# One transformer block in fp32 on one core: two projection sweeps of 16 steps rewritten as one hand-ordered pipeline of 32 steps

## Chip, cores and metric

The kernel runs on 1 core of one Trainium2 chip, as one launch. The metric is device time in microseconds (us), taken as the median of several executions. Engine names are those of the profile: PE is the matrix engine (PEld its weight loads), DVE the vector engine, ACT the scalar engine, POOL the general engine, SP the engine that issues nearly all DMAs.

## The reference

One trunk layer of a diffusion backbone: 512 latent tokens of width 2048, and 256 context tokens that only give keys and values. The conditioning vector `c` gives six shift, scale and gate vectors, `mod = silu(c) @ w_ada + b_ada`. In short:

```
h = rmsnorm(x) * (1 + scale1) + shift1
q, k, v, cb, cc, ch = split(h @ w_in)
attn = softmax attention of 8 query heads over 512 latent and 256 context keys
conv = cb * conv3(cc * ch)
x = x + gate1 * concat(rmsnorm(attn), rmsnorm(conv)) @ w_o
h2 = rmsnorm(x) * (1 + scale2) + shift2
x = x + gate2 * (silu(g) * a) @ w_down      where a, g = split(conv3(h2 @ w_up))
out = rmsnorm(x)
```

Each matrix product is made of three passes over a high and a low part of both operands (high by high, low by high, high by low), so that it comes out near full fp32 precision.

## The kernel before

Everything is held transposed: 128 channels on the partitions, 512 tokens along the free axis. The width of 2048 is 16 channel tiles (`KT`). Weights come from HBM as `wr` tiles, ACT casts them to the high part `wh` (line 107), DVE or POOL subtracts to get the low part `wl` (line 108), and PE runs three passes (`mm3s`, line 142).

The stage that the change touches is the first. Seven PSUM banks collect seven output tiles at a time while the loop runs over the 16 input tiles. **Sweep 1** (from line 339) does this with `x * scale1` for the seven query tiles before the RMS factor of a token is known; the factor is multiplied in later (line 410). **Sweep 2** (from line 399) does it with the finished `h` for two key tiles and five convolution tiles. A step of a sweep needs:

- its weights, 448 KB, a `load_w`: cast and subtraction;
- one column of `scale1` (sweep 1) or `shift1` (sweep 2) for its channel tile. This is a dot product of `c` with 1 MB of `w_ada` (`w_ap`): `columns_load` fetches it, `row_sums` does 32 small matmuls on PE (line 170), ACT copies the sums out (line 173), `row_cols` turns them with two more (line 177), and DVE adds the bias (`mod_cols`, lines 321 and 324);
- in sweep 2 a DVE product `hm = x * scale1 * rstd` (line 401) and a shift with a split into high and low, one ACT and one DVE instruction (lines 241, 242).

PE's order is written out by hand: `row_sums` of the next step, seven high by high matmuls, `row_cols`, seven with the low weights, seven with the low activations. The order of DVE and ACT is a planner's, made from modelled times. SP issues in order and waits where a buffer is not yet free. `fetch_w` and `fetch` chain the DMAs behind one another while `strict` is set, and loosely after it is cleared, which happens at the first step of sweep 2.

The other 64 columns of `mod` come from rows of `w_ada` that DVE multiplies with `sil = silu(c)`, spread over all partitions: two halves of 512 KB and two dots per row (line 181). This is `ada2`, which takes the next row from `rest`. Two rows are done in sweep 1, eight in sweep 2, 28 in the projections after it, 12 in the attention and 14 in the output projection (`merge`, one row per tile while there are any). The row tiles in the sweeps share four buffers (`ar`) with `w_ap`. `sil` itself is made at the start: `c` comes as four rows of one partition (`crow`), PE multiplies each by a column of ones (line 335), and ACT takes the SiLU (line 336).

Between the sweeps the seven banks are copied out by ACT (line 394), and the RMS factor `rx` is spread over the partitions by a PE product with `ones` (line 228).

Of the kernel before, what the change touches and what calls it, by code (L numbers as in the profile page):

```python
# [10 lines left out]
F32 = mybir.dt.float32  # L11
# [5 lines left out]
P = 128  # L17
# [33 lines left out]
def tile_hybrid_block(ctx: ExitStack, tc: tile.TileContext, a: dict, out: bass.AP):  # L51
# [251 lines left out]
    with tc.tile_pool(name="xpl", bufs=16) as xpl:  # L303
        def row(ap):
            return ap.rearrange("(o k) -> o k", o=1)

# [10 lines left out]
        def mod_cols(j, rows):  # L317
            o = gb[:, 2 * P:2 * P + 2]
            row_cols(o, rows)
            if j < 16:  # L320
                dve.tensor_scalar(out=mod2[:, j, :], in0=o, scalar1=col("b_ada", j), scalar2=None,
                                  op0=ADD)
            else:
                dve.tensor_scalar(out=mod2[:, j, :], in0=o, scalar1=b1[:, j - 16:j - 15],
                                  scalar2=col("norm1_w", j - 16), op0=ADD, op1=MUL)
# [11 lines left out]
        xt = []  # L337
        acc, rx = kraw[1], rstd_c

        def load_x(k):  # L340
            if k < KT:
                x = xpl.tile([P, T], F32, tag="x", name="x")
                fetch(x, a["x"][:, k])
                xt.append(x)

        def start_cols():
            sp.dma_start(out=cols, in_=a["cols"])
            o = COFF["b_ada"] + 16
            dve.tensor_scalar(out=b1, in0=cols[:, o:o + KT], scalar1=1.0, scalar2=None, op0=ADD)

        g0 = [psum(f"g0_{i}") for i in range(NQ)]
        gb = psum("gb")
        late.append(start_cols)
        sq = 0

        XK, SK = ({11: 3, 9: 3, 8: 3, 1: 2, 0: 2, 2: 2}, 10)
        for k in range(KT):
            if not k:
                ws = load_w(a["w_g0"][0], NQ * P)
                row_ = mod_load(16)  # L360
                load_x(0)
                sp.dma_start(out=ident, in_=a["ident"])
                mod_cols(16, row_sums(gb, row_, s32))
            sc = scale_col(k)
            x = xt[k]
            act.activation(r(hh[k]), x, AF.Identity, scale=sc)
# [12 lines left out]

            rows = row_sums(gb, row_, s32) if k + 1 < KT else None  # L380

            def between(k=k, rows=rows):
                if rows is not None:
                    mod_cols(17 + k, rows)
                else:
                    rstd_spread(q, NT, gb, rx)
            mm3s([(g0[i], k == 0, k == KT - 1, wh[:, i * P:(i + 1) * P],
                   wl[:, i * P:(i + 1) * P], hh[k], hl[k]) for i in range(NQ)], False, between)
            if k == SK:
                q = rstd_sums(acc, NT, D, gb[:, 3 * P:3 * P + 8])  # L390
        row_ = mod_load(0)
        for i in range(NQ):
            qraw[i] = big(f"q{i}")
            act.copy(qraw[i], g0[i])

        g0 = [psum(f"g1_{i}") for i in range(7)]
        gb = psum("gb")
        mod_cols(0, row_sums(gb, row_, s32))
        for k in range(KT):
            t = tmp("hm")  # L400
            dve.scalar_tensor_tensor(out=t, in0=xt[k], scalar=scale_col(k), in1=rx,
                                     op0=MUL, op1=MUL)
            shift_split(t, mod2[:, k, 0:1], hh[k], hl[k])
            wh, wl = load_w(a["w_g1"][k], 7 * P)
            if k + 1 < KT:
                row_ = mod_load(k + 1)
            if k % 2 == 1:
                ada2(1, ar4_tile)
# [920 lines left out]
```

## Time and profile before

| | |
|---|---|
| median of 3 executions | 2314.49 us (2313.19 to 2315.17) |
| the profiled execution | 2319.26 us, span of its trace 2317.5 us |
| PE busy | 2249.9 us, 97% of the span |
| DVE, ACT, POOL busy | 1219.3, 750.2, 381.3 us |
| mean granted PE clock | 0.985 of full speed |
| sweep 1 and sweep 2, first matmul of the first step to the next stage | 17.1 to 118.3 us, 127.8 to 249.9 us |

The profile is one execution as the hardware recorded it. The views used below are: busy time of each engine in chosen stretches (with the granted clock, as a part of 1, and what the DMAs moved), the instructions in order of time, who waited for whom, and groups of instructions with count and mean duration. A merged line of the timeline such as "x7" is several instructions in a row; matmuls overlap in the pipe, so the distance from start to start tells their cost, not the duration of one.

### The profile page before, as it was taken

The page shows a single profiled execution, that of the slowest core. Times are in us where ns is not written, and L with a number is a line of the kernel's source. Part 1 is how long each engine was busy: PE and PEld are TensorE (multiplying, and loading weights), DVE is VectorE, ACT ScalarE, POOL GpSimd, SP SyncE. Part 2 cuts the span into 40 slices and gives each one's busy share as a digit, 9 for nine tenths or more (in the row PEclk, how much of TensorE's full clock was granted, in tenths as well). Part 3 has the DMA queues.
Part 4 walks back from the last instruction along what each step waited for, and adds up shares of the span by engine and source line. Part 5 has one row for each costly group of instructions (what it writes and reads, how often), then busy time and mean ns, then how long its engine had stood idle before and what let it go on. Part 6 is the DMA issues. An engine that isn't in the chain of part 4 may idle for free. (4 is left out here: it accounts for less than half of the span.)

```text
span 2317.5 us, 28700 instructions
## 1 busy us (share of the span) xinstructions
PE 2249.9 (97%) x11446; PEld 1853.2 (80%) x11446; DVE 1219.3 (53%) x1683; ACT 750.2 (32%) x1028; POOL 381.3 (16%) x236
## 2 busy tenths in 40 slices
PE   9988999999999989999999999999999999999997
PEld 6766887777888767888888888888888888888887
DVE  3454557876888778643443434343443434343346
ACT  4322433334553333522323232322322232322324
POOL 0000000003444563210101010110101011110105
PEclk9989999999999999999999999999999999999999
DMA  9677778973554755433333333333233333333334
GB/s 360 242 239 256 240 227 284 304 236 116 166 178 159 270 177 172 128 96 100 92 99 100 92 99 98 94 99 100 91 100 99 92 100 95 97 100 96 96 100 155
DMA packets 110814, 350.33 MB, mean 151 GB/s; under 512 B 12756, under 2 KB 17108, under 8 KB 110680
## 3 DMA queue, kind: packets, MB, share of 16 engines
q1 hardware_dynamic: 108760, 345.88, 46.2%
q10 hardware_dynamic: 1920, 2.62, 0.4%
q8 instruction: 89, 1.46, 0.3%
q14 instruction: 45, 0.37, 0.0%
HBM read 335.60 MB, written 10.22 MB: 149 GB/s over the span
## 5 line engine op out<-in xcount | busy, mean ns | idle before, releaser
L108 DVE TENSOR_TENSOR wl<-wr,wh 128x1024 fp32r<-128x1024 f32 (+1 forms) x344 | 417.9, 1215 | 614.0 <-PE up L142 444.3
L107 ACT CAST wh<-wr 128x1024 fp32r<-128x1024 f32 (+2 forms) x392 | 405.3, 1034 | 991.4 <-PE up L142 474.6
L142 PE MATMUL up<-hh,wl 128*128 128x512 f32 x1312 | 324.0, 389 | 0.0
L142 PE MATMUL up<-hh,wh 128*128 128x512 f32 x1312 | 324.0, 389 | 0.0
L142 PE MATMUL up<-hl,wh 128*128 128x512 f32 x1312 | 324.0, 389 | 0.0
L142 PEld LDWEIGHTS up<-hh,wh 128*128 128x128 f32 x1312 | 246.3, 188 | 51.1
L142 PEld LDWEIGHTS up<-hh,wl 128*128 128x128 f32 x1312 | 246.3, 188 | 51.1
L142 PEld LDWEIGHTS up<-hl,wh 128*128 128x128 f32 x1312 | 246.3, 188 | 51.1
L1190 DVE SCALAR_TENSOR_TENSOR xs<-dn,mod,xs 128x512 f32<-128x512 f32 (+1 forms) x192 | 135.3, 705 | 225.7 <-PE dn L142 225.6
L1091 POOL TENSOR_TENSOR ua<-ua,ug 128x512 f32<-128x512 f32 x44 | 58.5, 1329 | 1103.2 <-ACT ug L1090 1103.2
L142 PE MATMUL dn<-fh,wh 128*128 128x512 f32 (+1 forms) x768 | 191.9, 372 | 0.0
L142 PE MATMUL dn<-fl,wh 128*128 128x512 f32 (+1 forms) x768 | 191.6, 371 | 0.0
L142 PE MATMUL dn<-fh,wl 128*128 128x512 f32 (+1 forms) x768 | 191.6, 371 | 0.0
L142 PEld LDWEIGHTS dn<-fh,wh 128*128 128x128 f32 x768 | 137.9, 188 | 25.0
L142 PEld LDWEIGHTS dn<-fh,wl 128*128 128x128 f32 x768 | 137.8, 188 | 24.9
L142 PEld LDWEIGHTS dn<-fl,wh 128*128 128x128 f32 x768 | 137.8, 188 | 24.9
L108 POOL TENSOR_TENSOR wl<-wr,wh 128x1024 fp32r<-128x1024 f32 (+1 forms) x48 | 116.8, 2436 | 165.8 <-ACT wh L107 113.0
L1098 POOL TENSOR_TENSOR fl<-ua,fh 128x512 fp32r<-128x512 f32 x44 | 97.6, 2218 | 38.5 <-ACT fh L1097 38.5
L217 POOL TENSOR_TENSOR rq<-rv,half 128x4 f32<-128x4 f32 (+2 forms) x11 | 15.9, 1459 | 497.7 <-DVE rv L213 494.1
L181 DVE CUSTOM_DVE_ANT_0 ar<-ar,sil,cols 128x1024 f32<-128x1024 f32 x50 | 63.9, 1279 | 45.5 <-DMA ar<-in_w_ada_dram 36.4
L181 DVE CUSTOM_DVE_ANT_0 ar<-ar,sil,acc 128x1024 f32<-128x1024 f32 x50 | 67.5, 1349 | 17.3 <-DMA ar<-in_w_ada_dram 15.5
L142 PE MATMUL pj<-hh,wl 128*128 128x512 f32 x272 | 68.1, 393 | 2.5 <-DVE wl L108 2.5
(307 smaller groups left out, 2851.3 us busy)
## 6 DMA issues: line engine op xcount, KB each, us to landing
wr<-in_w_up_dram SPq DMA_DIRECT2D x164, 512.0 KB, 3.6
ar<-in_w_ada_dram SPq DMA_DIRECT2D x100, 512.0 KB, 5.2
wr<-in_w_dn_dram SPq DMA_DIRECT2D x96, 512.0 KB, 3.5
ar<-in_w_ap_dram SPq DMA_DIRECT2D x48, 512.0 KB, 6.9
wr<-in_w_in_dram SPq DMA_DIRECT2D x40, 512.0 KB, 4.9
wr<-in_w_o_dram SPq DMA_DIRECT2D x32, 512.0 KB, 4.2
wr<-in_w_g_dram SPq DMA_DIRECT2D x32, 448.0 KB, 6.4
wr<-in_w_ada_dram SPq DMA_DIRECT2D x28, 512.0 KB, 4.7
```

The lines of the kernel that those rows point to most:

```text
L107: act.copy(r(wh[:, :n]), wr[:, :n])
L108: (eng or dve).tensor_tensor(out=r(wl[:, :n]), in0=wr[:, :n], in1=wh[:, :n], op=SUB)
L142: pe.matmul(ps, r(ops[a_]), r(ops[b_]), start=start and n == 0, stop=stop and n == 2)
L181: dve.tensor_tensor_reduce(out=wr, in0=wr, in1=s[:, si], op0=MUL, op1=ADD, scale=1.0, scalar=acc[:, i - 1:i] if i else col("b_ada", j), ac ...
L217: pool.tensor_tensor(out=q[:, i:e], in0=v[:, i:e], in1=half[:, :e - i], op=POW)
L1091: pool.tensor_tensor(out=ua, in0=ua, in1=ug, op=MUL)
L1098: pool.tensor_tensor(out=r(lo), in0=ua, in1=hi, op=SUB)
L1190: dve.scalar_tensor_tensor(out=x, in0=ps, scalar=mod[:, 80 + m:81 + m], in1=x, op0=MUL, op1=ADD)
```

## The change

- The two sweeps become one loop of 32 steps `g`. PE's order within a step stays (only step 0 starts with its seven first matmuls, before the row sums of step 1).
- DVE and ACT follow the order of the program until step 31 is done; the planner no longer places their work.
- Loads are issued three steps ahead (`w_load(g + 3)`, `mod_load(g + 3)`), all in one strict order until the end of step 31.
- The activations of step g + 1 and the cast of the weights of step g + 2 are done in step g, also where sweep 1 goes over to sweep 2. The seven banks are finished and copied out one after the other in step 15.
- Six rows of `w_ada` are done in the sweeps instead of ten: two in sweep 1, four in sweep 2. The latter four use the tiles of `x` as buffers (four DMAs of 256 KB a row), as these come free. The list `rest` goes on as before, so that the planned 28 and 12 rows follow, `merge` does 16 and the gate loop of the FFN the last two.
- `sil` is loaded by one DMA that reads `c` once for each partition, issued at step 6; ACT takes the SiLU in two halves in steps 8 and 9. The four rows, the eight matmuls and the four SiLUs at the start are gone.
- The first DMA behind `c2` is the 1 MB of `w_ap` for step 0, ahead of the first weights.

The diff, cut to what is spoken of:

```diff
-        def mod_load(j):
-            if j < 16:
-                return columns_load(a["w_ap"][j], ar4_tile, 1024)
-            if j % 2:
-                return columns_load(a["w_ap"][j], ar4_tile, 1024)
-            return columns_load(a["w_ap"][j], lambda: big("aq"), 512)
-
...
+        def w_load(g):
+            if g < 2 * KT:
+                raw[g] = wr_tile()
+                src = a["w_g0"][g] if g < KT else a["w_g1"][g - KT]
+                fetch_w(raw[g][:, :NQ * P], src)
+
+        def w_hi(g):
+            if g < 2 * KT:
+                wh = wp.tile([P, 1024], F32, tag="wh", name="wh")
+                act.copy(r(wh[:, :NQ * P]), raw[g][:, :NQ * P])
+                wt[g] = wh
+
+        def w_lo(g):
+            if g < 2 * KT:
+                wl = wp.tile([P, 1024], F32, tag="wl", name="wl")
+                n, wr, wh = NQ * P, raw.pop(g), wt[g]
+                dve.tensor_tensor(out=r(wl[:, :n]), in0=wr[:, :n], in1=wh[:, :n], op=SUB)
+                wt[g] = wh, wl
+
+        def make_hm(g):
+            if KT <= g < 2 * KT:
+                hm[g] = tmp("hm")
+                dve.scalar_tensor_tensor(out=hm[g], in0=xt[g - KT], scalar=scale_col(g - KT),
+                                         in1=rx, op0=MUL, op1=MUL)
+
+        def make_h(g):
+            k = g % KT
+            if g < KT:
+                sc = scale_col(k)
+                act.activation(r(hh[k]), xt[k], AF.Identity, scale=sc)
+                w_hi(g + 1)
+                dve.scalar_tensor_tensor(out=r(hl[k]), in0=xt[k], scalar=sc, in1=hh[k],
+                                         op0=MUL, op1=SUB)
+            else:
+                b, t = mod2[:, k, 0:1], hm.pop(g)
+                act.activation(r(hh[k]), t, AF.Identity, bias=b)
+                w_hi(g + 1)
+                make_hm(g + 1)
+                dve.scalar_tensor_tensor(out=r(hl[k]), in0=t, scalar=b, in1=hh[k],
+                                         op0=ADD, op1=SUB)
+
+        def ada_load(tile_, w):
+            j = rest.pop(0)
+            fa = sm.tile([P, 4], F32, tag="acc", name="acc")
+            fn = chain_dot(mod, j, sil, fa)
+            n = D // w
+            for i in range(n):
+                wr = tile_()
+                fetch(wr, a["w_ada"][j - 32, :, w * i:w * (i + 1)])
+
+                def dot(wr=wr, i=i):
+                    fn(wr, slice(i * w, (i + 1) * w), i, i == n - 1)
+                    if i == n - 1 and 64 <= j < 80:
+                        scale1(mod[:, j:j + 1], col("norm2_w", j - 64))
+                dots.append((dot, w))
+
+        def dot(w):
+            while dots and w >= dots[0][1]:
+                w -= dots[0][1]
+                dots.pop(0)[0]()
+
...
+        sweeps = ExitStack()
+        EN = mybir.EngineType
+        sweeps.enter_context(tc.manual_schedule(engines={EN.DVE, EN.Activation}))
...
-        crow = [big("row") for _ in range(4)]
-        for j in range(4):
-            sp.dma_start(out=crow[j][0:1, :], in_=row(a["c"][j * T:(j + 1) * T]))
-        sp.dma_start(out=pick, in_=a["pick"])
-        for j in range(4):
-            ps = psum("cb")
-            pe.matmul(ps, ones[0:1, :], crow[j][0:1, :], start=True, stop=True)
-            act.activation(sil[:, j * T:(j + 1) * T], ps, AF.Silu)
+        rows_ = {0: mod_load(0)}
+        fetch(cols, a["cols"])
+        fetch(pick, a["pick"])
+        load_x(1)
+        w_load(0)
+        rows_[1] = mod_load(1)
+        w_load(1)
+        load_x(2)
+        fetch(ident, a["ident"])
+        w_load(2)
+        rows_[2] = mod_load(2)
...
-        XK, SK = ({11: 3, 9: 3, 8: 3, 1: 2, 0: 2, 2: 2}, 10)
-        for k in range(KT):
-            if not k:
-                ws = load_w(a["w_g0"][0], NQ * P)
-                row_ = mod_load(16)
-                load_x(0)
-                sp.dma_start(out=ident, in_=a["ident"])
-                mod_cols(16, row_sums(gb, row_, s32))
-            sc = scale_col(k)
-            x = xt[k]
-            act.activation(r(hh[k]), x, AF.Identity, scale=sc)
-            dve.scalar_tensor_tensor(out=r(hl[k]), in0=x, scalar=sc, in1=hh[k], op0=MUL, op1=SUB)
-            wh, wl = ws
-            if k + 1 < KT:
-                ws = load_w(a["w_g0"][k + 1], NQ * P)
-                row_ = mod_load(17 + k)
-            for _ in range(XK.get(k, 1)):
-                load_x(len(xt))
-            if k in (11, 13):
-                ada2(1, ar4_tile)
-            while sq < len(xt) - 1 or sq < KT and len(xt) == KT:
-                add_square(acc, xt[sq], sq == 0, eng=dve)
-                sq += 1
-
...
+        mod_cols(0, row_sums(gb, rows_.pop(0), s32))
+        act.activation(r(hh[0]), xt[0], AF.Identity, scale=scale_col(0))
+        w_hi(0)
+        dve.scalar_tensor_tensor(out=r(hl[0]), in0=xt[0], scalar=scale_col(0), in1=hh[0],
+                                 op0=MUL, op1=SUB)
+        w_lo(0)
+        w_hi(1)
+
+        XN = {0: 1, 1: 1, 2: 2, 3: 2, 4: 2, 5: 2, 6: 2, 7: 1}
+        SN = {2: 3, 3: 2, 4: 2, 5: 2, 6: 2, 7: 2, 8: 2, 9: 1}
+        AD = {9: (ar4_tile, 1024), 11: (ar4_tile, 1024), 19: (x_tile, 512), 22: (x_tile, 512),
+              25: (x_tile, 512), 28: (x_tile, 512)}
+        DT = (11, 13, 21, 24, 27, 30)
+        SK, last = 10, 2 * KT - 1
+        added = 0
+        for g in range(2 * KT):
+            k = g % KT
+            if g == KT:
+                banks = [psum(f"g1_{i}") for i in range(NQ)]
+            wh, wl = wt.pop(g)
+
+            def group(n, i):
+                w, h = ((wh, hh[k]), (wl, hh[k]), (wh, hl[k]))[n]
+                pe.matmul(banks[i], r(w[:, i * P:(i + 1) * P]), r(h),
+                          start=k == 0 and n == 0, stop=k == KT - 1 and n == 2)
+
+            def group7(n):
+                for i in range(NQ):
+                    group(n, i)
+
+            if g == 0:
+                group7(0)
+            if g < last:
+                rows = row_sums(gb, rows_.pop(g + 1), s32)
+            w_load(g + 3)
+            if g + 3 <= last:
+                rows_[g + 3] = mod_load(g + 3)
+            load_x(XN.get(g, 0))
+            if g in AD:
+                ada_load(*AD[g])
+            if g == 6:
+                fetch(sil, a["c"].partition_broadcast(P))
+            w_lo(g + 1)
+            added = square_add(added)
+            if g in DT:
+                dot(1024)
+            square(SN.get(g, 0))
+            if g in (8, 9):
+                c_ = sil[:, (g - 8) * 1024:(g - 7) * 1024]
+                act.activation(c_, c_, AF.Silu)
+            group7(1 if g == 0 else 0)
+            if g < last:
+                mod_cols(g + 1, rows)
+                make_h(g + 1)
+            if g in DT:
+                dot(1024)
+            if KT < g <= KT + NQ:
+                dve.tensor_tensor(out=qraw[g - KT - 1], in0=qraw[g - KT - 1], in1=rx, op=MUL)
+            if g == SK + 1:
+                q = rstd_cols(gb[:, 3 * P:3 * P + 8:2], NT, D)
+            if g == SK + 2:
+                dg = diag(q, NT)
+            if g == KT - 1:
+                for i in range(NQ):
+                    group(1, i)
+                    group(2, i)
+                    qraw[i] = big(f"q{i}")
+                    act.copy(qraw[i], banks[i])
+                continue
+            if g:
+                group7(1)
+            if g == KT - 2:
+                pe.matmul(gb, ones, dg, start=True, stop=True)
+                act.copy(rx, gb)
+                make_hm(KT)
+            group7(2)
+            if g == SK:
+                for t in range(NT):
+                    pe.matmul(gb[:, 3 * P + 2 * t:3 * P + 2 * t + 2], acc[:, t * P:(t + 1) * P],
+                              ones[:, :2], start=True, stop=True)
+        sweeps.close()
+        strict[0] = False
+        g0 = banks
     ab = ctx.enter_context(ExitStack())
     kvp = ab.enter_context(tc.tile_pool(name="kvp", bufs=1, reuse_waits="tile"))
```

## Rows read from the trace of the kernel before

**Rows 1.** The page: busy time of PE, share of the span and instructions.
```profile
PE 2249.9 (97%) x11446; PEld 1853.2 (80%) x11446; DVE 1219.3 (53%) x1683; ACT 750.2 (32%) x1028; POOL 381.3 (16%) x236
```

**Rows 2.** Busy time by stretches: stretch, its length, engines (instructions), clock, DMA share, GB/s.
```profile
24.00:118.25 94.25, 94.00 (x802) 73.96 (x801) 45.70 (x73) 35.28 (x60) 1.01 (x1) 1.00 0.81 300
...
127.79:249.92 122.13, 106.51 (x818) 81.84 (x815) 56.20 (x87) 31.51 (x50) 0.00 (x0) 0.92 0.78 259
```

**Rows 3.** PE in order of time: start, duration, instruction, count, idle before and its releaser.
```profile
23.96 1.08 PE L170 MATMUL gb<-aq,s 128*32 128x128 f32 x32
...
30.21 1.08 PE L170 MATMUL gb<-ar,s 128*32 128x128 f32 x32
...
118.25 1.08 PE L170 MATMUL gb<-ar,s 128*32 128x128 f32 x32
...
127.79 2.82 PE L142 MATMUL g<-hh,wh 128*128 128x512 f32 x7
...
193.21 1.08 PE L170 MATMUL gb<-ar,s 128*32 128x128 f32 x16 [6.40 <-DMA ar<-in_w_ap_dram]
...
245.03 1.89 PE L142 MATMUL g<-hh,wh 128*128 128x512 f32 x7
...
249.92 1.98 PE L142 MATMUL pj<-hh,wh 128*128 128x512 f32 x8
```

**Rows 4.** Waits of PE from 0 to 250 us: total us, times, longest.
```profile
PE gb L170 <- DMA ar<-in_w_ap_dram: 16.3, 6, 6.4
PE gb L170 <- DVE mod L321: 4.4, 2, 4.0
```

**Rows 5.** DVE and ACT in order of time, between the sweeps.
```profile
117.00 3.52 ACT L394 COPY q<-g 128x512 f32<-128x512 f32 x7 [1.24 <-PE g L142]
...
120.44 4.30 DVE L410 TENSOR_TENSOR q<-q,rstd_c 128x512 f32<-128x512 f32 x7
...
125.66 0.21 DVE L321 TENSOR_SCALAR mod<-gb,cols 128x2 f32<-128x2 f32 x1
```

**Rows 6.** Waits of SP's queue, 118 to 250 us.
```profile
SPq L126 <- DVE acc L181: 32.8, 8, 5.3
```

**Rows 7.** SP and PE in order of time, start of the kernel.
```profile
2.70 7.16 PE L335 MATMUL cb<-row,ones 1*128 1x512 f32 x8 [2.70 <-DMA row<-in_c_dram]
...
3.31 0.43 SPq L126 DMA_DIRECT2D aq<-in_w_ap_dram  x1
...
9.79 2.40 PE L170 MATMUL gb<-aq,s 128*32 128x128 f32 x32
...
17.09 3.36 PE L142 MATMUL g<-hh,wh 128*128 128x512 f32 x7
```

**Rows 8.** Busy time by stretches at the start, columns as in rows 2.
```profile
4.00:10.00 6.00, 6.00 (x11) 1.86 (x14) 1.18 (x2) 2.72 (x5) 0.00 (x0) 1.00 0.87 295
...
10.00:24.00 14.00, 11.75 (x93) 7.75 (x87) 5.54 (x8) 5.82 (x10) 0.00 (x0) 1.00 1.04 400
```

**Rows 9.** DVE's groups from 0 to 420 us: count, busy us, mean ns, idle before.
```profile
L108 DVE TENSOR_TENSOR wl<-wr,wh 128x896 fp32r<-128x896 f32 x32 | 34.8, 1089 | 30.8 <-ACT wh L107 30.7
L181 DVE CUSTOM_DVE_ANT_0 ar<-ar,sil,cols 128x1024 f32<-128x1024 f32 x25 | 32.0, 1281 | 39.7 <-DMA ar<-in_w_ada_dram 30.5 <-DMA r<-kraw 9.2
...
L401 DVE SCALAR_TENSOR_TENSOR hm<-x,mod,rstd_c 128x512 f32<-128x512 f32 x16 | 11.5, 748 | 1.2 <-ACT rstd_c L238 1.0
```

**Rows 10.** DMA issues: KB each, median us from issue to landing.
```profile
ar<-in_w_ap_dram SPq DMA_DIRECT2D x48, 512.0 KB, 6.9
```

**Rows 11.** DVE's groups from 765 to 890 us, in the output projection.
```profile
L181 DVE CUSTOM_DVE_ANT_0 wr<-wr,sil,cols 128x1024 f32<-128x1024 f32 x10 | 22.7, 2273 | 6.2 <-DMA wr<-in_w_ada_dram 6.2
...
L181 DVE CUSTOM_DVE_ANT_0 wr<-wr,sil,acc 128x1024 f32<-128x1024 f32 x10 | 16.4, 1643 | 0.1
```

**Rows 12.** DVE's busy time, last row of the output projection to the row sums behind it.
```profile
840.15:858.43 18.28, 14.75 (x27) 0.92 0.40 124
```

**Rows 13.** PE in order of time, the row sums behind the output projection.
```profile
858.57 1.05 PE L232 MATMUL st<-ones,junk 128*128 128x2 f32 x8 [1.83 <-DVE junk L258]
```

More of the change, by code (lines that the diff above doesn't have):

```diff
@@ L303, in tile_hybrid_block, with mod_load @@
     with tc.tile_pool(name="xpl", bufs=16) as xpl:
-        def row(ap):
-            return ap.rearrange("(o k) -> o k", o=1)
         def scale_col(k):
             return mod2[:, 16 + k, 0:1]
-        def mod_load(j):
-            if j < 16:
-                return columns_load(a["w_ap"][j], ar4_tile, 1024)
-            if j % 2:
-                return columns_load(a["w_ap"][j], ar4_tile, 1024)
-            return columns_load(a["w_ap"][j], lambda: big("aq"), 512)
-        def mod_cols(j, rows):
+        def mod_load(g):
+            src = a["w_ap"][(16 + g) % 32]
+            if g < KT and g % 2 == 0:
+                return columns_load(src, lambda: big("aq"), 512)
+            return columns_load(src, ar4_tile, 1024)
@@ new lines, in tile_hybrid_block, with x_tile, load_x @@
+        xt, hm, wt, raw, hold, sq = [], {}, {}, {}, {}, []
+        acc, rx = kraw[1], rstd_c
+        def x_tile():
+            return xpl.tile([P, T], F32, tag="x", name="x")
+        def load_x(n):
+            for _ in range(n):
+                x = x_tile()
+                fetch(x, a["x"][:, len(xt)])
+                xt.append(x)
+        def w_load(g):
[3 more added lines that the diff above has]
+                fetch_w(raw[g][:, :NQ * P], src)
@@ new lines, in tile_hybrid_block @@
+        dots = []
+        def ada_load(tile_, w):
[11 more added lines that the diff above has]
+                dots.append((dot, w))
@@ new lines, in dot, with square @@
+        def dot(w):
+            while dots and w >= dots[0][1]:
+                w -= dots[0][1]
+                dots.pop(0)[0]()
+        def square(n):
+            for _ in range(n):
+                if len(sq) < KT:
+                    if not sq:
+                        act.activation(acc, xt[0], AF.Square)
+                        sq.append(None)
+                        continue
+                    s = tmp("sq")
+                    act.activation(s, xt[len(sq)], AF.Square)
+                    sq.append(s)
@@ L327, in tile_hybrid_block, with square_add @@
+        def square_add(n):
+            for s in sq[n:]:
+                if s is not None:
+                    dve.tensor_tensor(out=acc, in0=acc, in1=s, op=ADD)
+            return len(sq)
+        sweeps = ExitStack()
+        EN = mybir.EngineType
+        sweeps.enter_context(tc.manual_schedule(engines={EN.DVE, EN.Activation}))
         sp.dma_start(out=s2, in_=a["c2"])
-        crow = [big("row") for _ in range(4)]
-        for j in range(4):
-            sp.dma_start(out=crow[j][0:1, :], in_=row(a["c"][j * T:(j + 1) * T]))
+        rows_ = {0: mod_load(0)}
@@ L391, in tile_hybrid_block @@
[L391 to L408, printed above, removed]
-            if 1 <= k <= NQ:
-                dve.tensor_tensor(out=qraw[k - 1], in0=qraw[k - 1], in1=rx, op=MUL)
-            if k == 0:
-                strict[0] = False
-            rows = row_sums(gb, row_, s32) if k + 1 < KT else None
-            def between(k=k, rows=rows):
-                if rows is not None:
-                    mod_cols(k + 1, rows)
-            mm3s([(g0[i], k == 0, k == KT - 1, wh[:, i * P:(i + 1) * P],
-                   wl[:, i * P:(i + 1) * P], hh[k], hl[k]) for i in range(7)], False, between)
@@ new lines, in tile_hybrid_block @@
+        fetch(cols, a["cols"])
[8 more added lines that the diff above has]
+        rows_[2] = mod_load(2)
+        o = COFF["b_ada"] + 16
+        dve.tensor_scalar(out=b1, in0=cols[:, o:o + KT], scalar1=1.0, scalar2=None, op0=ADD)
+        banks = [psum(f"g0_{i}") for i in range(NQ)]
+        gb = psum("gb")
+        mod_cols(0, row_sums(gb, rows_.pop(0), s32))
```

36 lines of the change are left out of this document (7 added, 29 removed).

## The prediction

> **What bounds it now.** I began with the page: PE is busy 97% of the span [rows 1], so only time that PE stands still or runs slowly can be won. The stretches say where that lies [rows 2]. In sweep 1 PE is busy 94.00 of 94.25 us at full clock; sweep 2, with the same count of matmuls, takes 122.13 us, is busy 106.51 and has a granted clock of 0.92. PE in order of time gives the measure: a step of sweep 1 takes 30.21 - 23.96 = 6.25 us from row sums to row sums, and a last step, which has none behind it, 249.92 - 245.03 = 4.89 us [rows 3]. Row sums alone take 1.08 us. Were sweep 2 to follow at once with that period, it would end at 118.25 + 1.08 + 15 x 6.25 + 4.89 = 217.97 us; it ends at 249.92. So **32.0 us** are lost, 8.5 between the sweeps (127.79 - 118.25 - 1.08) and 23.5 in sweep 2.
>
> The waits say by whom [rows 4]. Six times PE waits for a `w_ap` load, 16.3 us in all, up to 6.40 us at 193.21 us [rows 3]; the rest of the 23.5 is the half clock behind such a stall and short waits. These loads are late because SP, in order, stands in front of a buffer that a dot of `ada2` has not yet read: 32.8 us in eight waits [rows 6], one for each of the eight rows in sweep 2. Between the sweeps DVE is the cause: it runs seven `q` scalings in a row, 4.30 us from 120.44 us, before the bias at 125.66 us for which PE waits [rows 5].
>
> The 23.5 us come from starts of matmuls, not from PE's idle time, which is 122.13 - 106.51 = 15.6 us [rows 2]; the difference is slow clock that counts as busy. (The Trainium skill, "Perfetto Trace Analysis", "Identifying the Most-Contended Engine", says that matmul busy share is no good measure of the distance to the roofline, because matmuls are pipelined. Taken by busy share, sweep 2 would give 7.9 us less and the time would be 2291.9 us; the clock of 0.92 bears the rule out here.)
>
> **The change, part by part.**
>
> *Between the sweeps.* Step 16's activations are made in step 15 and the scalings are spread one to a step, so the 8.5 us go. What is late next are ACT's seven copies, 3.52 us [rows 5], now each behind its bank's last matmuls in step 15. The copy of step 17's row sums stands behind the seventh, and the last bank is needed about when it comes free. I charge 1 us; bounds 0 and 4, the latter what one stall cost before (below).
>
> *Sweep 2.* Per step SP issues the weights and two halves of `w_ap`, three steps ahead. Four `ar` buffers hold two steps, so a pair is issued when the row sums of step g + 1 are over, 1.1 us into step g, and is needed at the start of step g + 2: 2 x 6.25 - 1.1 = 11.4 us against 6.9 us from issue to landing [rows 10]. No dot shares these buffers in sweep 2 any more. Bytes: 1.51 MB a step and 1.05 MB for a row of `w_ada` every third, 1.86 MB in 6.25 us, 297 GB/s, where the stream has reached 400 [rows 8]. The four rows wait in SP for tiles of `x`, at steps 25 and 28 until the middle of the step or of the next; behind that wait stand only loads for two steps later, at 28 those of the next stage. DVE in the fullest step (21): subtraction 1.09, two dots 2.56, bias 0.21, `hm` and the low part 0.75 each, a scaling 0.61, together 5.97 of 6.25 us [rows 5, 9]; other dot steps lack the scaling. A waiting DVE or ACT instruction now holds back all behind it on its engine, but the activations are due 3 us before PE wants them and the low parts 5. So all 23.5 us go.
>
> *Sweep 1.* It had nothing to win; its two rows still share `ar`, where SP's wait ends within the step. The SiLUs in steps 8 and 9 (no row for this shape; about two casts of half the width, 1 us each) fit beside ACT's four other instructions.
>
> *The broadcast of `c`.* No row shows such a DMA. From below 1.05 MB at 400 GB/s, 2.6 us [rows 8]; from above two loads of half the size one after the other, 2 x 6.9 = 13.8 us [rows 10]. It is issued in step 6 behind step 9's loads and needed in the middle of step 8, over 12.5 us later. I take the first, as it is 128 runs of 8 KB, hidden; at the other end it costs 1 us.
>
> *Start.* Before, PE's eight products for `sil` (7.16 us from 2.70) and SP's small loads came first, and the first `w_ap` load was issued at 3.31 us, the row sums began at 9.79 and the first step at 17.09 [rows 7], step 1 at 23.96 [rows 3]. Now `w_ap` is issued 2 us earlier, and the first matmuls don't wait for the second column. The stream ran at 295 GB/s from 4.0 us, about 1 us behind the first large issue [rows 8]; from 2.2 us it brings the 2.03 MB of column, bias, first `x` and weights by 9.1. With the activation and the cast, some 2 us, the first step starts at 11.1. Its 21 matmuls took 6.87 us with the cold clock (17.09 to 23.96), the row sums of step 1 come between them at the cold 2.40 [rows 7]: step 1 at 20.4, **3.5 us** earlier. Bounds 1 and 6 (a stream a fifth slower; warm row sums and a faster chain).
>
> *Four rows of `w_ada` put off.* The projections and the attention do as many rows as before. `merge` does 16, two more, at its end. Such a row costs DVE 2.27 + 1.64 = 3.92 us there, 7.8 for both [rows 11], and from the last dot to the row sums DVE is busy 14.75 of 18.28 us [rows 12]: 3.5 free, and PE waits 1.83 us for DVE at that point already [rows 13]. I charge **4 us**; bounds 0 (the dots slip behind the sums) and 8 (all of it). Their four loads also stand in the `wr` buffers ahead of the next weights, which is part of the upper bound. The two rows in the gate loop I cost at nothing: DVE is idle 47% of the span [rows 1]; without that cover they are 4 x 1.28 = 5.1 us [rows 9].
>
> *Sum:* 32.0 + 3.5 - 1 - 4 = **30.5 us**. The profiled execution took 2319.26 us (span 2317.5), 4.8 above the median; it would take 2288.8, the median 2314.49 - 30.5 = **2284.0**. With the bounds: 32 + 6 = 38 gives 2276.5, 32 + 1 - 4 - 8 = 21 gives 2293.5. The planner also lays the later stages anew; what that does no row tells, and I let the range carry a few us for it.
>
> **Rivals.**
>
> *Stalls at the rows (2293 to 2306).* The four rows of sweep 2 are in the strict order, 1.05 MB each, and behind them everything waits. Before, six stalls cost 16.3 us idle [rows 4] and 7.9 of slow clock, 4.0 each; four would give back 16: 2300. For it: SP's waits for dots were the cause before, and SP now waits for `hm` at steps 25 and 28. Against: the 11.4 us of lead and 297 of 400 GB/s.
>
> *Late in every step (slower).* The lead of two steps is too short: with four buffers the period is half of landing time plus 1.1 us. From a landing of 11.4 us on this costs, and from 14.9 us on (a period of 8.0, 16 x 1.8 = 28 us and the slow clock behind each stall) it eats the gain. At 17 us the period is 9.05 and the loss 45 us: 2284 + 45 = 2329. For it: DVE and ACT can no longer be moved around a late load. Against: 6.9 us [rows 10].
>
> *The order was not the cause (no change).* If loads come late for a reason in the memory, 23.5 us stay, half of the hand-over too, and the rows in `merge` eat the start: 2311. Against: sweep 1, with more bytes a second (300 against 259 GB/s [rows 2]), has no stall.
>
> **How the numbers follow.** Forecast 0.78, stalls at the rows 0.15, no change 0.03, slower 0.04. A measurement of this kernel tells 0.2% (4.6 us) from no change. Faster: 0.78 + 0.15 = 0.93; same 0.03; slower 0.04. The range takes the forecast's bounds, 3 us below for the later stages, and most of the stalls: 2273 to 2302.
>
> **What would show it.** Right: in the changed trace the row sums follow each other by 6.25 us through all 32 steps, the first at about 20 us, the projection's first matmul at about 215 us, no PE wait for `w_ap`, clock 1.00 from 24 us on, and a PE wait before the row sums behind the output projection of some 6 us instead of 1.83. Wrong: PE waits for `w_ap` at steps 21 to 31 (stalls), a period over 7 us in sweep 2 (late in every step), or a projection that starts at 215 us and a time over 2300, when later stages gave the gain back.

## The result, and the profile after

The changed kernel takes 2287.22 us (median of 4 runs, 2283.14 to 2292.19), the kernel before 2313.84 on the same chip: a ratio of 0.9885 (95% interval 0.986 to 0.9911), 1.15% faster. The forecast was 2284.0, in a range of 2273 to 2302. The profiled execution took 2292.19 us, 27.1 less than that of before (2319.26); the traces are compared against this difference.

The page, PE's line [rows 1]:
```profile
PE 2233.5 (98%) x11438; PEld 1842.9 (80%) x11438; DVE 1222.7 (53%) x1699; ACT 747.9 (33%) x1026; POOL 383.6 (17%) x236
```
Busy time by stretches, columns as in [rows 2]: step 1 to step 15, from there to the projections, then output projection, first products with `w_u`, gate loop.
```profile
18.76:108.45 89.69, 89.45 (x781) 69.93 (x780) 45.86 (x73) 36.59 (x62) 1.79 (x1) 1.00 0.88 324
108.45:213.17 104.72, 104.72 (x902) 82.57 (x902) 60.20 (x105) 35.43 (x59) 0.00 (x0) 1.00 0.85 291
706.20:814.80 108.60, 95.02 (x388) 75.65 (x386) 88.46 (x98) 29.90 (x41) 58.13 (x26) 0.93 0.70 239
814.80:894.60 79.80, 73.47 (x306) 57.59 (x306) 60.19 (x112) 29.72 (x43) 36.14 (x18) 0.98 0.51 159
894.60:987.10 92.50, 89.05 (x384) 73.25 (x385) 55.15 (x64) 40.65 (x52) 21.00 (x12) 0.98 0.44 138
```
The second line is the change's success: from step 15 on PE is busy in 104.72 of 104.72 us at full clock, where sweep 2 of before stood still and ran slowly [rows 2]. The last line is the opposite. The same stage of the kernel before, in the same view:
```profile
926.90:1014.00 87.10, 87.10 (x386) 72.14 (x385) 48.23 (x53) 40.16 (x52) 19.31 (x12) 1.00 0.38 119
```
It had no idle time there; it has 3.45 us now, and is 5.4 us longer.

PE in order of time, columns as in [rows 3]:
```profile
10.84 3.32 PE L459 MATMUL g<-hh,wh 128*128 128x512 f32 x7 [1.96 <-ACT wh L344]
14.09 1.08 PE L170 MATMUL gb<-ar,s 128*32 128x128 f32 x32
...
18.76 0.93 PE L170 MATMUL gb<-aq,s 128*32 128x128 f32 x24
...
108.45 1.08 PE L170 MATMUL gb<-ar,s 128*32 128x128 f32 x32
...
114.71 1.08 PE L170 MATMUL gb<-ar,s 128*32 128x128 f32 x32
...
202.25 1.08 PE L170 MATMUL gb<-ar,s 128*32 128x128 f32 x32
...
213.17 1.98 PE L142 MATMUL pj<-hh,wh 128*128 128x512 f32 x8
```
Step 0 begins at 10.84 us, step 1 at 18.76 and step 16 at 114.71, one period of 6.25 after step 15: no hand-over is left, and 202.25 - 114.71 is fourteen periods of 6.25. (Only step 1 and the two steps with extra products, 10 and 14, are longer: 6.74, 7.04 and 7.13 us.) The projections begin at 213.17 instead of 249.92. PE's waits from 0 to 230 us, as in [rows 4]. Of the 16.3 us for `w_ap` there 1.3 lie in step 0, at 14.89 us; the other 15.0, five waits in sweep 2, are gone (of the 5.5 here 4.21 lie ahead of the very first matmul, the rest at 5.89 and 19.92 us):
```profile
PE gb L170 <- DMA aq<-in_w_ap_dram: 5.5, 3, 4.2
PE g L459 <- ACT wh L344: 2.0, 1, 2.0
...
```

How far a profiled execution is ahead of that of before, at the start of each stage, in us:

| kernel | projections | output projection | `w_u` | `up` (gate loop) | `dn` | whole time |
|---|---|---|---|---|---|---|
| changed | 36.7 | 38.5 | 33.6 | 32.3 | 26.9 | 27.1 |
| after_again | 35.5 | 39.1 | 35.2 | 35.9 | 30.8 | 31.0 |
| gate_rows_later | 36.2 | 41.1 | 35.5 | 34.2 | 34.2 | 33.6 |
| four_rows_in_gate | 36.0 | 40.5 | 39.5 | 41.3 | 41.3 | 41.5 |
| half_merge_rows | 36.3 | 43.3 | 47.7 | 51.4 | 41.4 | 40.5 |
| rows_spread | 36.7 | 42.1 | 57.9 | 62.4 | 62.2 | 50.9 |
| rows_spread_8 | 36.9 | 38.8 | 54.0 | 57.6 | 57.7 | 46.3 |

The changed kernel wins 36.7 us in the sweeps, 1.8 more up to the output projection, and gives back 6.2 from there to the gate loop and 5.4 in it. Two profiles of this one kernel (the first two lines) differ by up to 3.9 us at a mark, and the first six lines, whose programs are the same up to the output projection, by 4.8 us there; smaller differences between two lines say nothing.

Where it gives back is seen in order of time. In the gate loop, DVE, SP and PE:
```profile
896.75 1.81 SPq L126 DMA_DIRECT2D wr<-in_w_ada_dram  x2
...
902.46 1.28 DVE L181 CUSTOM_DVE_ANT_0 wr<-wr,sil,cols 128x1024 f32<-128x1024 f32 x1 [2.99 <-DMA wr<-in_w_ada_dram]
...
906.60 0.75 DVE L242 SCALAR_TENSOR_TENSOR hl<-hm,mod,hh 128x512 fp32r<-128x512 f32 x1
907.41 0.50 PE L142 MATMUL up<-hl,wh 128*128 128x512 f32 x1 [3.43 <-DVE hl L242]
907.74 3.15 PE L142 MATMUL up<-hh,wl 128*128 128x512 f32 x8
```
A dot of `ada2` stands in DVE's order ahead of the last low part `hl`, and its load is not there yet. DVE waits 2.99 us for the row, works off its dots, then makes `hl`, for which PE has waited 3.43 us; the clock falls behind that gap (0.98 over the stage), which makes up the rest of the 5.4. This is no accident of one profile: six profiled kernels do the two rows in these passes (changed, after_again and four of the experiments below), and in each PE waits for `hl`, 2.3 to 3.6 us, and the gate loop gives back 4.3 to 6.5.

PE's waits in the three stages, 690 to 1000 us (`oa` is the output projection, `u` the products with `w_u`, `st` the row sums behind it), and ACT at the end of the output projection:
```profile
PE oa L142 <- ACT wh L107: 7.5, 3, 4.5
PE oa L142 <- POOL wl L108: 4.4, 2, 2.9
PE u L142 <- ACT wh L107: 3.9, 2, 2.2
PE up L142 <- DVE hl L242: 3.4, 1, 3.4
PE st L232 <- DVE junk L258: 2.4, 1, 2.4
```
```profile
813.91 0.83 ACT L107 CAST wh<-wr 128x768 fp32r<-128x768 f32 x1 [8.29 <-DMA wr<-in_w_u_dram]
```
In the same three stages of before these waits were:
```profile
PE oa L142 <- ACT wh L107: 6.8, 4, 2.5
PE oa L142 <- POOL wl L108: 2.5, 1, 2.5
PE u L142 <- ACT wh L107: 2.2, 1, 2.2
PE st L232 <- DVE junk L258: 1.8, 1, 1.8
```
They are each somewhat longer now, 4.9 us together, though waits of this size also differ between kernels with the same `merge` (the first is 9.6 us in before_no_rows). Most are for weights, not for the row sums: the four loads of the two further rows take turns with the weights in the `wr` buffers, and a cast for `w_u` waits 8.29 us for its load. What holds the weights up is seen in SP's queue, from 706 to 815 us:
```profile
SPq L120 <- DVE mod L181: 21.2, 10, 5.0
SPq L120 <- DVE acc L181: 16.6, 3, 8.0
```
SP waits with loads of weights (line 120) for buffers that a dot (line 181) has not read yet; before, from 745 to 848 us, these were 17.6 and 16.0 us. It is the kind of wait that the prediction saw in sweep 2.

### The profile page after: what moved, and what is told of

Same layout as the page of the kernel before. It is cut to its first block, busy times and chain, and to the rows that moved or that the text cites. A ratio compares the mean times of both kernels' runs of the same rounds, so it can differ in the third digit from the quotient of the medians.

```text
span 2290.4 us, 28675 instructions
## 1 busy us (share of the span) xinstructions
PE 2233.5 (98%) x11438; PEld 1842.9 (80%) x11438; DVE 1222.7 (53%) x1699; ACT 747.9 (33%) x1026; POOL 383.6 (17%) x236
## 5 line engine op out<-in xcount | busy, mean ns | idle before, releaser
L107 ACT CAST wh<-wr 128x1024 fp32r<-128x1024 f32 (+1 forms) x360 | 375.3, 1043 | 966.7 <-PE up L142 473.1
L108 DVE TENSOR_TENSOR wl<-wr,wh 128x1024 fp32r<-128x1024 f32 x312 | 383.8, 1230 | 575.0 <-PE up L142 436.7
L181 DVE CUSTOM_DVE_ANT_0 ar<-ar,sil,cols 128x1024 f32<-128x1024 f32 x42 | 53.8, 1281 | 33.3 <-DMA ar<-in_w_ada_dram 20.8
L142 PE MATMUL pj<-hh,wh 128*128 128x512 f32 x272 | 69.5, 397 | 0.0
```

What stands on the lines that cost most here:

```text
L107: act.copy(r(wh[:, :n]), wr[:, :n])
L108: (eng or dve).tensor_tensor(out=r(wl[:, :n]), in0=wr[:, :n], in1=wh[:, :n], op=SUB)
L142: pe.matmul(ps, r(ops[a_]), r(ops[b_]), start=start and n == 0, stop=stop and n == 2)
L181: dve.tensor_tensor_reduce(out=wr, in0=wr, in1=s[:, si], op0=MUL, op1=ADD, scale=1.0, scalar=acc[:, i - 1:i] if i else col("b_ada", j), ac ...
```

## The experiments

Theory: (1) in the kernel before, the eight rows of sweep 2, with their dots and loads in loose order, cost its 23.5 us; (2) in the changed kernel the gate loop's loss is the dot that waits for its load, not DVE's time; (3) in the output projection every row costs PE time by its loads. There are twelve runs in three groups; each ratio is to the kernel before, timed again with its group (2316.79, 2315.99 and 2316.87 us).

**after_again**: the changed kernel once more, for a second profile.

> The changed kernel once more, as the measure for the next three, which differ from it only behind the attention. Both theories: 2283 to 2292 us, median near 2287; the sweeps end near 213 us; PE waits some 3.4 us for a low part (hl) at the start of the up projections in at least some executions. Theory A: the give-back of some 10 us behind the sweeps comes from the four rows of w_ada that were put off (two in the gate loop, two in merge). Theory B: it is the scatter of those stages, whose order the planner lays anew, and the rows cost nothing by themselves.

Measured: 2287.64 us (2282.15 to 2288.26), ratio 0.9869 (0.9856 to 0.9882). The wait for `hl` is there again, 3.1 us, and the gate loop gives back 5.1. The two stages ahead of it give back 3.2 instead of 6.2.

**gate_rows_later**: the two rows of the gate loop go from its first two passes (counted 3 and 4 in the program) to passes 4 and 5.
```diff
-        ada2(-(-len(rest) // (6 - i)) if i < 6 else len(rest), wr_tile)
+        ada2(0 if i < 4 else -(-len(rest) // (6 - i)) if i < 6 else len(rest), wr_tile)
```


> The last two rows are done at i = 4 and 5 of the gate loop instead of 3 and 4, so that no dot stands in DVE's queue ahead of the last low part of h. Theory A: the PE wait of 3.4 us for hl and the slow clock behind it go, some 5 us less than the changed kernel, median near 2282. Theory B: within 2 us of the changed kernel.

Measured: 2285.78 us (2281.89 to 2287.02), ratio 0.9863 (0.985 to 0.9877). In the profile the wait for `hl` is gone and the gate loop gives back nothing (34.2 at both ends). The median is 1.9 us under after_again, with intervals that overlap: the mechanism is shown by the profile, its worth of 5 us is not shown by the times. (This profile lost 6.9 us ahead of the gate loop, more than the other two.)

**four_rows_in_gate**: as that, and the last two rows of `merge` are left to the gate loop as well.
```diff
-        ada2(1, wr_tile)
+        ada2(int(m < 14), wr_tile)
```


> As gate_rows_later, and merge does 14 rows as before the change; all four rows put off are done at i = 4 and 5 of the gate loop. Theory A: the lead over the kernel before stays 38 to 40 us from the attention to the end, another 4 to 7 us less, median near 2276. Theory B: within 2 us of the changed kernel, or the gate loop takes as much longer.

Measured: 2279.44 us (2277.38 to 2286.31), ratio 0.9844 (0.9828 to 0.986). Output projection and gate loop, columns as in [rows 2]:
```profile
704.20:808.90 104.70, 94.01 (x387) 75.68 (x386) 85.25 (x94) 30.99 (x43) 60.35 (x28) 0.94 0.69 234
...
885.60:972.70 87.10, 87.10 (x386) 72.10 (x385) 57.72 (x69) 39.05 (x52) 18.38 (x12) 1.00 0.51 164
```
The gate loop now has four rows instead of two and takes 87.10 us as before the change, without idle time, though DVE is busier (57.72 against 55.15 us). So its loss was one of order, not of DVE's time. The stages ahead of it gain 0.8 instead of losing 6.2 or 3.2.

**half_merge_rows**: `merge` does a row in every second call only; the gate loop does ten.
```diff
-        ada2(1, wr_tile)
+        ada2(m % 2, wr_tile)
...
-        ada2(-(-len(rest) // (6 - i)) if i < 6 else len(rest), wr_tile)
+        ada2({3: 0, 4: 3, 5: 3}.get(i, 4), wr_tile)
```


> merge does a row on every second tile (8 instead of 16), the other ten are done in the gate loop, three at i = 4, three at i = 5, four at i = 6. Theory A, a row in merge costs PE time because DVE is nearly full there: 8 rows less give back more than the two of four_rows_in_gate, 2264 to 2272. Rival to that: the gate loop has 8 dots per 22 us beside its own work and PE waits there instead, 2276 to 2290. Theory B: within 2 us of the changed kernel.

Measured: 2281.82 us (2277.06 to 2282.19), ratio 0.9845 (0.9831 to 0.9858), no better. From the output projection to the gate loop the lead grows by 8.1 us (43.3 to 51.4) where four_rows_in_gate had 0.8: 7.3 for six rows fewer in `merge`, 1.2 each. The gate loop then loses 10.0. Gate loop, and PE's longest waits in and behind it:
```profile
875.50:972.60 97.10, 89.53 (x384) 72.99 (x384) 73.89 (x92) 37.24 (x50) 18.07 (x12) 0.98 0.61 197
```
```profile
PE up L142 <- DVE wl L108: 5.4, 2, 3.6
...
PE dn L142 <- ACT wh L107: 2.2, 1, 2.2
```
Three and four rows a pass are too many: PE waits for the low part of a weight that DVE makes behind the dots.

**before_no_rows**: in the kernel before, sweep 2 does no row; the eight columns of `mod` are filled with ones.
```diff
-                ada2(1, ar4_tile)
+                j = rest.pop(0)
+                dve.memset(mod[:, j:j + 1], 1.0)
```


> The kernel before, without the eight rows of w_ada in sweep 2 (left out of the computation, a constant stands in their columns of mod). Theory C: SP's waits for these dots made the w_ap loads late, so PE's six waits of 16.3 us go and sweep 2 takes 99 to 103 us instead of 122; the hand-over of 9.5 us stays, and the projections start near 227 to 231 us instead of 250. Theory D: the planner's order of DVE and ACT is the cause, rows or not; sweep 2 stays above 112 us and the projections start above 238 us.

Measured: 2296.73 us (2293.47 to 2301.97), ratio 0.992 (0.9898 to 0.9942). Between the sweeps and sweep 2, columns as in [rows 2], then PE's waits, 0 to 250 us:
```profile
118.25:127.80 9.55, 3.35 (x68) 2.49 (x66) 8.72 (x15) 4.25 (x9) 0.00 (x0) 0.78 0.43 139
127.80:226.60 98.80, 98.80 (x822) 77.72 (x815) 38.09 (x55) 31.65 (x50) 0.00 (x0) 0.99 0.70 235
```
```profile
PE gb L170 <- DVE mod L321: 4.0, 1, 4.0
...
PE gb L170 <- DMA ar<-in_w_ap_dram: 1.3, 1, 1.3
```
Sweep 2 takes 98.80 us instead of 122.13: 23.3 of the 23.5 us are the rows'. The one wait for `w_ap` lies in step 0; sweep 2 has none. The hand-over stays, as nothing there was touched.

**before_strict**: in the kernel before, the fetches keep their strict order to the end of sweep 2.
```diff
-            if k == 0:
+            if k == KT - 1:
                 strict[0] = False
```


> The kernel before with the strict order of loads kept to the last step of sweep 2, all eight rows in it. If the buffers shared with dots are the cause of the stalls, they stay: sweep 2 over 112 us, projections from 240 to 252 us. Rival: the loose order let loads of later stages and of rows go ahead of w_ap; strict alone brings sweep 2 to 99 to 105 us and the start to 227 to 233 us.

Measured: 2305.45 us (2301.97 to 2310.1), ratio 0.9948 (0.9931 to 0.9964). Sweep 2, then PE's waits, 0 to 250 us, then SP's, 118 to 240:
```profile
127.80:238.30 110.50, 103.41 (x819) 79.02 (x816) 56.82 (x88) 31.12 (x51) 0.00 (x0) 0.96 0.86 306
```
```profile
PE gb L170 <- DVE mod L321: 6.8, 2, 4.8
PE gb L177 <- ACT rs L173: 3.6, 4, 1.4
PE gb L170 <- DMA ar<-in_w_ap_dram: 3.1, 4, 1.3
...
```
```profile
SPq L126 <- DVE acc L181: 34.9, 8, 6.1
```
SP waits for the dots as long as before (34.9 against 32.8 us [rows 6]), yet PE's waits for `w_ap` fall from 16.3 to 3.1 us (in sweep 2 alone from 15.0 to 1.8). The strict order alone brings the projections 11.6 us forward, half of what the rows cost. In the half that is left PE waits mostly for DVE and ACT; why these are late was not tested. Neither theory's number came out.

**rows_in_wap_buffers**: in the changed kernel the four rows share the `w_ap` buffers again.
```diff
-        AD = {9: (ar4_tile, 1024), 11: (ar4_tile, 1024), 19: (x_tile, 512), 22: (x_tile, 512),
-              25: (x_tile, 512), 28: (x_tile, 512)}
+        AD = {9: (ar4_tile, 1024), 11: (ar4_tile, 1024), 19: (ar4_tile, 1024), 22: (ar4_tile, 1024),
+              25: (ar4_tile, 1024), 28: (ar4_tile, 1024)}
```


> The changed kernel, but the four rows of sweep 2 are loaded into the four ar buffers that w_ap uses (two DMAs of 512 KB) instead of the tiles of x. Theory C: SP again waits for dots in front of w_ap loads; PE waits for w_ap some 2 to 5 us at each of the four rows, the projections start at 218 to 233 us. Rival: the strict order three steps ahead absorbs it, start at 213 to 215 us.

Measured: 2290.8 us (2289.81 to 2293.78), ratio 0.9891 (0.9871 to 0.991). PE has one wait for `w_ap` in this sweep, and the projections begin at 214.7 us. That wait, and SP's waits for the rows:
```profile
PE gb L170 <- DMA ar<-in_w_ap_dram: 1.1, 1, 1.1
```
```profile
SPq L126 <- DVE mod L181: 9.4, 3, 3.6
```
SP does stand in front of the dots' buffers again, for 9.4 us, but PE hardly feels it; whether the lead of three steps, the strict order or the smaller number of rows takes it up, this run does not tell. One step takes 7.58 us instead of 6.25: the buffers in `x` are worth 1.3 us here, not the whole gain.

**after_planner_order**: the changed kernel with DVE and ACT placed by the planner again.
```diff
-        sweeps.enter_context(tc.manual_schedule(engines={EN.DVE, EN.Activation}))
```


> The changed kernel with DVE and ACT left to the planner in the sweeps; loads, buffers and the order of the program as in the change. Theory C: loads and buffers were the cause of the stalls in sweep 2; the projections start at 213 to 221 us, at most the hand-over (some 5 us) comes back. Theory D: the fixed order is what removed them; stalls return, start at 230 us or later.

Measured: 2291.0 us (2285.1 to 2291.23), ratio 0.9887 (0.9867 to 0.9907). The period in sweep 2 stays within 0.02 us of 6.25 but for one step of 6.37, and the projections begin at 214.1 us, inside the 213.2 to 214.5 of the table's first six lines. In the sweeps the fixed order as such is worth no more than 0.1 us.

**lead_two**: loads two steps ahead instead of three.
```diff
-        w_load(2)
-        rows_[2] = mod_load(2)
...
-            w_load(g + 3)
-            if g + 3 <= last:
-                rows_[g + 3] = mod_load(g + 3)
+            w_load(g + 2)
+            if g + 2 <= last:
+                rows_[g + 2] = mod_load(g + 2)
```


> The changed kernel with loads issued two steps ahead instead of three. If the lead is what keeps PE from waiting: a w_ap load is then issued some 1 us into step g and needed at the start of step g + 1, 5.2 us against 5.4 us from issue to landing, so PE waits 0.5 to 2 us in most steps and the projections start at 220 to 250 us. Rival: the loads land in time because nothing else stands in the queue; start at 212 to 216 us.

Measured: 2290.77 us (2285.63 to 2293.12), ratio 0.988 (0.9865 to 0.9895). One place is late, 96.5 to 98.4 us, with 1.4 us in three waits; two steps are longer by 0.9 and 1.3 us, 2.2 together, and the projections begin at 215.8, 2.7 us later.

**after_old_start**: the changed kernel with the old way to `sil`.
```diff
+        crow = [big("row") for _ in range(4)]
+        for j in range(4):
+            sp.dma_start(out=crow[j][0:1, :],
+                         in_=a["c"][j * T:(j + 1) * T].rearrange("(o k) -> o k", o=1))
...
+        for j in range(4):
+            ps = psum("cb")
+            pe.matmul(ps, ones[0:1, :], crow[j][0:1, :], start=True, stop=True)
+            act.activation(sil[:, j * T:(j + 1) * T], ps, AF.Silu)
...
-            if g == 6:
-                fetch(sil, a["c"].partition_broadcast(P))
...
-            if g in (8, 9):
-                c_ = sil[:, (g - 8) * 1024:(g - 7) * 1024]
-                act.activation(c_, c_, AF.Silu)
```


> The changed kernel with sil made at the start as before (four rows of c, eight matmuls, four SiLUs), without the broadcast DMA. If the start was worth the 5.2 us that the trace shows (step 1 at 18.8 instead of 24.0 us), the first step's matmuls start at 13 to 15 us and the projections at 216 to 219 us. Rival: the small loads and products hide beside the 1 MB load that comes anyway, start within 1 us of 213 us.

Measured: 2287.74 us (2285.44 to 2289.71), ratio 0.9879 (0.9861 to 0.9896). The first matmul of step 0 comes at 14.56 us instead of 10.84, step 1 at 22.42 instead of 18.76, the projections at 216.3, 3.1 later. In after_again these are 11.37, 20.52 and 214.5, so the price lies between 1.9 and 3.7 us. In the whole time it can't be told from the changed kernel.

**rows_spread**: the rows are spread further: `merge` does six, passes 4 to 6 of the gate loop two each, the first down projection one at each of its first six steps.
```diff
-        ada2(1, wr_tile)
+        ada2(int(m in (0, 1, 4, 7, 10, 13)), wr_tile)
...
-        ada2(-(-len(rest) // (6 - i)) if i < 6 else len(rest), wr_tile)
+        ada2(2 if i in (4, 5, 6) else 0, wr_tile)
...
-            down((i - 2) // CH - 1)
+            down((i - 2) // CH - 1,
+                 hooks={m2: [lambda: ada2(1, wr_tile)] for m2 in range(6)} if i == 6 else {})
```


> The changed kernel with the 18 rows behind the attention spread anew: merge does 6 (tiles 0, 1, 4, 7, 10, 13), the gate loop two each at i = 4, 5, 6, and the first down projection six, one behind each of its first six pairs of tiles. Theory A with the price that half_merge_rows gave (about 1.7 us of PE time for each row in merge, none for two a pass of the gate loop): ten rows less in merge give 17 us on four or five rows at the start of the up projections, and nothing is lost behind them if DVE has room in the down projection; 2262 to 2272. Rival: DVE or the row loads hold up the down projection as they did the gate loop with three and four rows, 2275 to 2285.

Measured: **2269.69 us** (2268.36 to 2272.27), ratio 0.9793 (0.978 to 0.9807). This beats both kernels: 47.2 us less than the kernel before, timed with it. Output projection, `w_u`, gate loop and the beginning of `dn`:
```profile
702.60:790.50 87.90, 87.90 (x387) 72.47 (x386) 58.63 (x66) 32.84 (x45) 55.54 (x29) 1.00 0.59 192
790.50:864.50 74.00, 71.19 (x308) 56.53 (x307) 55.58 (x105) 26.83 (x38) 31.20 (x16) 1.00 0.51 158
864.50:951.80 87.30, 87.30 (x384) 72.08 (x385) 63.35 (x80) 38.04 (x51) 18.03 (x12) 1.00 0.57 184
951.80:1000.00 48.20, 41.47 (x165) 32.74 (x164) 34.89 (x46) 9.46 (x11) 2.78 (x2) 0.93 0.67 216
```
The output projection takes 87.90 us at full clock instead of 108.60, and the gate loop does six rows in 87.30. The first down projection is the new place of loss (62.2 us of lead at its start, 51.0 at its end). There PE waits 6.7 us in four waits, one of them here, in order of time:
```profile
954.14 1.28 DVE L181 CUSTOM_DVE_ANT_0 wr<-wr,sil,cols 128x1024 f32<-128x1024 f32 x1 [3.13 <-DMA wr<-in_w_ada_dram]
955.35 1.22 DVE L108 TENSOR_TENSOR wl<-wr,wh 128x1024 fp32r<-128x1024 f32 x1
956.63 2.08 PE L142 MATMUL dn<-fh,wl 128*128 128x512 f32 x4 [2.85 <-DVE wl L108]
```
It is the chain of the gate loop again: a dot waits for its row ahead of a low part.

**rows_spread_8**: as that, with eight rows in the sweeps (six of them in steps 19 to 29, every second) and four in `merge`.
```diff
-        AD = {9: (ar4_tile, 1024), 11: (ar4_tile, 1024), 19: (x_tile, 512), 22: (x_tile, 512),
-              25: (x_tile, 512), 28: (x_tile, 512)}
-        DT = (11, 13, 21, 24, 27, 30)
+        AD = {9: (ar4_tile, 1024), 11: (ar4_tile, 1024)}
+        AD.update({g: (x_tile, 512) for g in range(19, 30, 2)})
+        DT = (11, 13, 21, 23, 25, 27, 29, 31)
...
-        ada2(1, wr_tile)
+        ada2(int(m in (2, 5, 8, 11)), wr_tile)
```


> As rows_spread, with eight rows in the sweeps instead of six (one every second step from 19 to 29, loads into the tiles of x) and four in merge. DVE would be busy some 10 of 12.5 us in two steps of sweep 2 and the stream move 326 of 400 GB/s, so the sweeps should keep their period and the projections start at 213 to 215 us; two rows less in merge: 2 to 4 us under rows_spread. Rival: the loads come late, PE waits for w_ap in sweep 2 and the start is past 217 us.

Measured: 2273.0 us (2270.93 to 2277.61), ratio 0.9809 (0.9795 to 0.9823), no gain over rows_spread. The sweeps bear the two rows (projections at 213.0 us, every step of sweep 2 6.25 us), but the lead is 3.3 us smaller ahead of the output projection, within what two profiles of one kernel differ by.

## Why the prediction was right, point by point

The median came out 3.2 us above the forecast of 2284.0. That is closer than the terms are: against the profile three came out better than forecast, by 4.6 us together, and three worse, by 8.2. That they cancel to 3.6 is luck. The largest term, the 32.0 us of hand-over and sweep 2, was read from start to start of the row sums and needs no reason for the stalls; it held, while the reason given held in part. The terms, in us (their sum is 26.9, the last mark but one in the table):

| term | predicted | measured | how |
|---|---|---|---|
| hand-over and sweep 2 | 32.0 - 1 | 32.1 | step 16 to the projections: (249.92 - 119.33) - (213.17 - 114.71) |
| start | 3.5 | 5.2 | 23.96 - 18.76; 3.4 in the second profile |
| sweep 1 | 0 | -0.6 | step 1 to 16: 95.37 before, 95.95 now |
| projections and attention | 0 | 1.8 | 38.5 - 36.7; within the scatter |
| two more rows in `merge` | -4 | -6.2 | 32.3 - 38.5; -3.2 in the second profile |
| two rows in the gate loop | 0 | -5.4 | 26.9 - 32.3; -5.1 in the second |

**Sweep 2.** The size was right: 23.3 us by before_no_rows, 23.5 predicted. The reason, that SP stands in front of a dot's buffer, is a part of it only. With the strict order alone SP waits as long and half of the loss is gone; with shared buffers in the changed kernel nearly nothing comes back. So "No dot shares these buffers" was not what the gain needed. Undoing the fixed engine order, the `x` buffers or the third step of lead costs 0.1, 1.3 and 2.2 us of step time in the sweeps: none of them carries the gain by itself, and that they cover for each other is likely but not shown. The strict order alone is not enough (before_strict). Whether four rows instead of eight, or the place of their dots in the program, would be was not tried; six rows still keep the period (rows_spread_8). The rivals "stalls at the rows" and "late in every step" fall with the period of 6.25 us in every step of sweep 2.

Two readings behind the 32.0 were off without moving it: sweep 2 had five stalls of 15.0 us, not six of 16.3, and the 8.5 us between the sweeps hold the row sums of step 17 (1.1 us), which are work of sweep 2.

**Hand-over.** The 1 us for ACT's seven copies was not lost.

**Start.** Step 0 began at 10.84 us, 11.1 predicted, and the 21 matmuls took 6.84 (18.76 - 10.84 - 1.08), as predicted. Of the 1.7 us by which the term was too small, 0.3 lie in step 0's start and 1.3 in the row sums of step 1, 1.08 us instead of 2.40. But that belongs to this profile: in after_again these row sums take 1.94 us and step 1 begins at 20.52, the 20.4 of the prediction. Over the ten profiles with this start it begins at 18.76 to 20.52 us. after_old_start, at 22.42, puts 1.9 to 3.7 us of the term on the old way to `sil`; the rest lies in the new order.

**The broadcast of `c`** landed 8.8 us after its issue, between the bounds of 2.6 and 13.8, the SiLUs took 1.05 us each; both stayed hidden, as costed.
```profile
sil<-in_c_dram SPq DMA_DIRECT2D x1, 1024.0 KB, 8.8
```

**The rows in `merge`.** The size was about right: the seven profiled kernels with 16 rows there lose 3.2 to 7 us of lead from the output projection to the gate loop, and of the three others with 14, before_no_rows and before_strict lose 1.8 and 3.1 and four_rows_in_gate gains 0.8, on average 4 us apart. But the sign I named for it was wrong: PE's wait before the row sums is 2.38 us and 0 to 2.4 in the other six, not some 6 (1.83 before [rows 13]). I took the price for DVE's time at the end of the stage; it is paid at the weights, which come later because rows' loads stand in their buffers until the dots are done. DVE's time is in that too (it is busy 88.46 of 108.60 us), and its share and that of the loads were not separated. With eight rows in `merge` instead of fourteen the way to the gate loop is 7.3 us shorter, and with six, in other places, 19.5 (20.3 - 0.8). How much of the last figure is the number and how much the places was not separated.

**The rows in the gate loop** are the step that failed: "The two rows in the gate loop I cost at nothing: DVE is idle 47% of the span". The cover named is an average of busy time; a dot that waits for its load is not busy, and holds all that is behind it. It cost 5.4 us; gate_rows_later removes it with the same two rows, four_rows_in_gate with twice as many. That the prediction's price without cover, 5.1 us, is so near is chance: it is the dots' DVE time, and four_rows_in_gate has twice that time at no loss.

## What to carry over

An idle share is no cover for work in an in-order engine: ask for each added instruction what it waits for, and what that a faster engine needs stands behind it. A side load that takes turns with the weights in their buffers has a price there too, as it holds its buffer until its arithmetic is done; it is best put where the engines wait for nothing, a few at a time. When a gain has one size and several parts that could each give it, undo them one by one before naming the cause, and put each alone into the old kernel as well: parts that cover for each other show little when one is missing.

## What the runs showed of the hardware that was not expected

The row sums of step 1, the first behind seven matmuls, begin at 14.09 to 14.87 us in the ten profiles of the new start and take 1.08 to 1.94 us for the same 32 products, where 2.40 was the price of the first in the kernel before [rows 7]. And one load that gives the same 8 KB to all 128 partitions, 1.05 MB, took 8.8 us to land, where loads of half that size in the same stretch, 40 to 75 us, had a median of 6.9:
```profile
ar<-in_w_ap_dram SPq DMA_DIRECT2D x4, 512.0 KB, 6.9
```
The four times of the changed kernel lie in two pairs, 2283.14 and 2283.59, 2290.84 and 2292.19; what makes the difference was not found.
